# A hybrid decoder trunk: forget sums carried into the scores by the keys' zero rows, the mask inside the minimum, query blocks taken last to first

## The chip, the cores and the metric

One Trainium2 chip, one of its cores. A time is the device time of one execution in microseconds (us), as the core's own clock gives it. Three executions of the kernel before took 1271.95, 1272.39 and 1273.62 us; 1272.39 is their median. A separate, profiled execution gives the trace. TensorE is PE in the profile, its weight load PEld, VectorE DVE, ScalarE ACT, GpSimd POOL, and SyncE SP (here it only issues DMAs).

## What is computed

Two decoder layers over 16 meta tokens and 512 real ones (T = 528 columns, features on the partitions), width 1024. In each layer one input projection feeds eight heads of forgetting attention (64 features each) and four retention heads (128 features each); their outputs go through one output projection, then a gated feed-forward part follows. The change lies in the attention:

```python
c = jnp.cumsum(logf, axis=1).transpose(0, 2, 1)          # one running sum for each head
s = jnp.einsum('bhqd,bhkd->bhqk', q_blk, k_).astype(jnp.float32) * scale
s = s + c_q[..., :, None] - c_k[..., None, :]
s = jnp.where(k_pos[None, :] <= q_pos[:, None], s, -jnp.inf)
p = jax.nn.softmax(s, axis=-1)
return jnp.einsum('bhqk,bhkd->bhqd', p.astype(v_.dtype), v_)
```

A softmax over keys is not changed by a term that is the same for all keys of a query, so the kernel needs only the keys' sums `c_k`. The four real query blocks hold 128 queries each; block b (0 to 3) reads 16 + 128 (b + 1) keys: 144, 272, 400 or 528. The meta queries are block -1 (16 queries, 16 keys), present in layer 0 alone, since layer 1 drops the meta outputs.

## The kernel before

All products use fp32 split into a rounded high part and the remainder (`split`, L142: ACT rounds, DVE subtracts), so a dense product is three matmuls (L218), in layer 0 on two halves of 264 columns, in layer 1 on 512 columns where meta columns aren't needed. Weights come by SP's DMA queue into three buffers `raw`, are rounded by ACT (L192) and subtracted by POOL or DVE (L195) one or two jobs ahead.

The order of PE is written out by hand: `layer` (L1247) builds a list of steps, and `merge` (L247) puts placed steps between base steps, a place being the number of the base step that it stands behind. The order of DVE, ACT, POOL and SP follows from a scheduler at build time, and each of these engines works strictly in that order; PSUM tiles for the placed steps come from a pool of four (`psum_a`, L260).

The front of layer 0 (L1316): the first dense steps of q and k of head pair 0, interleaved (16 steps, `qk`), then `first_parts`, the gates' matmuls (L381), the sums of squares (L291) that give R, the row norm (L296 to L301), then the delayed ends of q and k (`q_done`, `k_done`) around `forget_sums`, then v. `forget_sums` (L391) makes the running sum by a scan (L401), writes it to DRAM (`cdr`, L403), and the first `scores` step of each head reads one row of it back to all 128 partitions (`bc`, L501). Both DMAs stand in SP's queue, between the loads of weights.

`fox_steps` (L474) are the placed steps of one head pair g: for each of its two heads s, and for block -1, 0, 1, 2, 3 in that order, `scores` then three steps later `turn`; `values` after the second score; `product(0)` and `product(1)`. In detail:

- `q_done` (L430): `qs` of head s holds the rounded queries in the head's 64 rows and their remainder in the other 64.
- `k_done` (L444): `kh` holds the rounded keys in both halves; `kl` the keys' remainder in the head's half, zero in the other half (zeroed once for each layer, L85). Two matmuls (L511) with `qs` then give all three terms.
- `scores` (L496): the two matmuls for each segment, the mask added to the diagonal 128 columns in PSUM by DVE (L517), one DVE instruction that takes `bc` minus score, writes it and its minimum (L518), and ACT's Exp (L531) with the row's sum. Block 3 has 528 keys and so two segments of 264, two PSUM tiles and two L518.
- `turn` (L550): PE transposes the block's weights (L420), ACT and DVE split them into `pth` and `ptl` (L143, L144).
- `product` (L569): the products with values (L584) over five groups of keys j = 0 to 4; group j = 0 spans all 512 query columns and stands first.

A group's placed steps stand between the dense steps of retention head g and of head pair g + 1; for g = 0 the scores begin behind base step 7 and end at 31 (L1329). The end of the program (L1178 to L1231) takes the final norm over the last 240 columns: squares on ACT, their sum on DVE, split, five matmuls with ones (L1159), a root, three DVE instructions, four output multiplies (L1137), with DMAs to the output.

Of the kernel before, what the change touches and what calls it, by code (L numbers as in the profile page):

```python
# [10 lines left out]
F32 = mybir.dt.float32  # L11
F32R = mybir.dt.float32r
# [27 lines left out]
def hybrid_kernel(ctx, tc, x_t, w_in, w_fl, w_out, w_gate, w_up, w_down, vecs, b_fg, rope, decay, mask, ident, out_t):  # L40
# [13 lines left out]
    msk = const.tile([128, 128], F32, name="msk")  # L54
# [12 lines left out]
    p_tiles, t_tiles, pm_tiles, v_tiles, end_tiles, low_keys = [], [], [], [], [], []  # L67
# [13 lines left out]
    def enter_att(l):  # L81
        enter("att")
        low_keys[:] = [phase["att"].tile([128, T], F32R, name=f"kl{s}") for s in range(2)]
        for s, t in enumerate(low_keys):
            (nc.gpsimd if l else nc.vector).memset(t[64 * (1 - s):64 * (2 - s)].bitcast(F32), 0.0)  # L85
# [283 lines left out]
    def forget_gates(l, st):  # L369
        if l:  # L370
            load_gates(l, st)
            gate_weights(l, st)
        else:
            for t, src in ((bfg, b_fg), (msk, mask), (idt, ident)):
                nc.sync.dma_start(t, src)
        wf = st["wf"]
# [14 lines left out]
    def forget_sums(l, st):  # L391
# [10 lines left out]
        st["cdr"] = tc.dram_tile([FH, T], F32, name=f"cdr{l}")  # L402
        nc.sync.dma_start(st["cdr"], z2)  # L403
# [20 lines left out]
    def fox_dense(l, g, ly, real, st):  # L424
# [5 lines left out]
        def q_done(ps):  # L430
# [4 lines left out]
            for s in range(2):  # L435
# [3 lines left out]
                nc.scalar.copy(sv(t, real, a0, a1), sv(tq, real, a0, a1))  # L439
                nc.vector.tensor_sub(sv(t, real, b0, b1), sv(tq, real, a0, a1), sv(t, real, a0, a1).bitcast(F32))  # L440
                st["q"].append(t)


        def k_done(ps):  # L444
# [3 lines left out]
            for s in range(2):  # L448
                kh = at(f"kh{s}")
                kl = low_keys[s]  # L450
                a0, a1 = ROWS[s]
                for b0, b1 in (ROWS[s], ROWS[1 - s]):
                    nc.scalar.copy(kh[b0:b1, :], tk[a0:a1, :])
                nc.vector.tensor_sub(kl[a0:a1, :], tk[a0:a1, :], kh[a0:a1, :].bitcast(F32))
                st["k"].append((kh, kl))
# [18 lines left out]
    def fox_steps(g, st, ly, real):  # L474

        blocks = list(range(0 if real else -1, NBLK))
# [19 lines left out]
        def scores(s, b):  # L496
            nq, nk, q0 = span(b)
            if b == blocks[0]:
                bc = at("bc", F32, bufs=2)
                hd = 2 * g + s  # L500
                nc.sync.dma_start(bc, ly["cdr"][hd:hd + 1, :].partition_broadcast(128))  # L501
                st["bc"] = bc
            bc = st["bc"]
# [4 lines left out]
            for c0, c1 in segs:  # L508
                sc = psum_a()
                for i, kk in enumerate(st["k"][s]):  # L510
                    nc.tensor.matmul(sc[0:nq, 0:c1 - c0], st["q"][s][:, q0:q0 + nq], kk[:, c0:c1],  # L511
# [913 lines left out]
```

## Time and profile before

| | us |
|---|---|
| median of three executions | 1272.39 |
| lowest, highest | 1271.95, 1273.62 |
| span of the profiled execution, first to last instruction | 1270.1 |
| what lies around the span (median less span) | 2.3 |
| PE busy in the span | 1252.6 (99%) |
| DVE, ACT, POOL busy | 1003.8, 694.5, 263.3 |
| granted TensorE clock, mean of the span | 0.996 |

The profiled execution is another than the three timed ones; its own time is known as its span, and the 2.3 us around it is taken from the median. A busy PE isn't a PE at its peak, as matmuls overlap: one that is issued every 0.12 us shows 0.28 us. So PE's waits are read from the list of who waited for whom, from the timeline, and from the granted clock in a stretch. The chain that ended last, the part 4 of the page, follows the work back from the last instruction.

### The profile page before, as it was taken

What the parts mean: (1) busy time and instruction counts of PE and PEld (TensorE: products, weight loads), DVE (VectorE), ACT (ScalarE), POOL (GpSimd) and SP (SyncE); (2) the same over time, 40 slices, a digit from 0 to 9 for tenths busy, and PEclk for the clock granted to TensorE, in tenths of its full rate; (3) what the DMA queues carried; (4) which work ended last, traced back from release to release, by engine and by line L of the source; (5) the groups of instructions that cost most, each with busy time, mean ns of one, the idle gap of its engine ahead of it and who ended that gap; (6) DMA issues with size and microseconds to landing.
All of it is one profiled execution on the core that took longest, in us unless ns stands there. A gap on an engine that the chain in (4) does not pass through costs nothing.

```text
span 1270.1 us, 23589 instructions
## 1 busy us (share of the span) xinstructions
PE 1252.6 (99%) x9225; PEld 1193.1 (94%) x9225; DVE 1003.8 (79%) x1866; ACT 694.5 (55%) x1284; POOL 263.3 (21%) x524
## 2 busy tenths in 40 slices
PE   9999999999999999999999999999999999999997
PEld 8899999999999999999998989998789999999996
DVE  7877856879988888887786877568899888888867
ACT  7666556676444444444465665457764444444445
POOL 3355546420000000000025546454100000000000
PEclk9999999999999999999999999999999999999999
DMA  6322222213323232322323122221223333333321
GB/s 218 93 68 84 83 94 75 68 68 116 106 96 100 100 100 100 100 100 84 101 76 114 63 101 84 77 91 67 100 91 126 101 100 101 100 100 100 100 84 67
DMA packets 45679, 120.56 MB, mean 95 GB/s; under 512 B 5360, under 2 KB 12272, under 8 KB 45568
## 3 DMA queue, kind: packets, MB, share of 16 engines
q1 hardware_dynamic: 45136, 118.77, 28.3%
q8 instruction: 72, 1.18, 0.4%
q14 instruction: 39, 0.32, 0.1%
q10 hardware_dynamic: 432, 0.29, 0.1%
HBM read 116.91 MB, written 2.13 MB: 94 GB/s over the span
## 4 chain that ended last, share of the span: by engine, by line
PE 89%; DVE 5%; ACT 4%; DMA 1%; issue 1%; ACTq 0%; DVEq 0%; SPq 0%
PE psd L218 27%; PE psa L902 18%; PE psd L1037 14%; PE psd L902 13%; PE psa L218 5%; PE psa L1037 4%; PE psa L420 2%; PE psa L511 1%; PE psa L584 1%; PE psa L717 1%; PE psa L751 1%; DMA bc<-cdr 1%; PE psa L381 1%; ACT whi L192 1%; DVE pr L518 0%
## 5 line engine op out<-in xcount | busy, mean ns | idle before, releaser
L195 POOL TENSOR_TENSOR wlo<-raw,whi 128x128 fp32r<-128x128 f32 x504 | 259.1, 550 | 288.8 <-ACT whi L192 287.3
L218 PE MATMUL psd<-xh,whi 128*128 128x264 f32 (+1 forms) x792 | 195.6, 314 | 0.4 <-ACT whi L192 0.4
L218 PE MATMUL psd<-xl,whi 128*128 128x264 f32 (+1 forms) x792 | 186.3, 302 | 0.6 <-DVE xl L321 0.6
L218 PE MATMUL psd<-xh,wlo 128*128 128x264 f32 (+1 forms) x792 | 186.7, 303 | 0.0
L218 PEld LDWEIGHTS psd<-xh,whi 128*128 128x128 f32 x792 | 128.2, 189 | 5.2 <-ACT whi L192 0.8
L218 PEld LDWEIGHTS psd<-xh,wlo 128*128 128x128 f32 x792 | 127.0, 188 | 6.3 <-DVE wlo L195 0.6
L218 PEld LDWEIGHTS psd<-xl,whi 128*128 128x128 f32 x792 | 127.6, 189 | 5.2 <-DVE xl L321 1.2
L192 ACT CAST whi<-raw 128x512 fp32r<-128x512 f32 (+1 forms) x168 | 98.2, 613 | 45.7 <-PE psd L218 31.5
L890 ACT CAST whi<-raw 128x1024 fp32r<-128x1024 f32 (+2 forms) x62 | 54.8, 884 | 50.3 <-PE psd L902 37.0
L890 ACT CAST fwhi<-raw 128x1024 fp32r<-128x1024 f32 (+2 forms) x62 | 55.6, 897 | 47.9 <-PE psd L902 40.1
L891 DVE TENSOR_TENSOR fwlo<-raw,fwhi 128x1024 fp32r<-128x1024 f32 (+2 forms) x62 | 64.0, 1032 | 11.7 <-ACT fwhi L890 11.6
L85 POOL MEMSET kl<- 64x528 f32 x2 | 1.1, 534 | 345.5 <-PE psa L902 345.5
L891 DVE TENSOR_TENSOR wlo<-raw,whi 128x1024 fp32r<-128x1024 f32 (+2 forms) x62 | 62.9, 1014 | 12.2 <-ACT whi L890 12.1
L902 PE MATMUL psa<-th,whi 128*128 128x264 f32 (+1 forms) x232 | 65.4, 282 | 0.0
L902 PE MATMUL psa<-th,wlo 128*128 128x264 f32 (+1 forms) x232 | 65.4, 282 | 0.0
L902 PE MATMUL psa<-tl,whi 128*128 128x264 f32 (+1 forms) x232 | 65.3, 282 | 0.0
L902 PE MATMUL psa<-th,fwhi 128*128 128x264 f32 (+1 forms) x224 | 63.4, 283 | 0.0
L902 PE MATMUL psa<-tl,fwhi 128*128 128x264 f32 (+1 forms) x224 | 63.3, 283 | 0.0
L902 PE MATMUL psa<-th,fwlo 128*128 128x264 f32 (+1 forms) x224 | 63.2, 282 | 0.0
L531 ACT ACTIVATE pr<-pr,nmax 128x144 f32<-128x144 f32 (+1 forms) x64 | 36.9, 576 | 43.2 <-DVE nmax L518 31.2
L890 ACT CAST fwhi<-S 128x1024 fp32r<-128x1024 f32 x20 | 21.0, 1049 | 68.6 <-PE psa L902 66.5
L968 ACT COPY e<-psa 128x264 f32<-128x264 f32 (+1 forms) x114 | 42.9, 376 | 27.7 <-PE psa L902 23.6
(356 smaller groups left out, 4036.6 us busy)
## 6 DMA issues: line engine op xcount, KB each, us to landing
raw<-w_in SPq DMA_DIRECT2D x54, 512.0 KB, 3.5
raw<-w_gate SPq DMA_DIRECT2D x44, 512.0 KB, 4.0
fraw<-w_up SPq DMA_DIRECT2D x38, 512.0 KB, 3.4
raw<-w_down SPq DMA_DIRECT2D x64, 256.0 KB, 2.7
raw<-w_out SPq DMA_DIRECT2D x16, 512.0 KB, 3.4
raw<-w_down SPq DMA_DIRECT2D x32, 192.0 KB, 2.5
bc<-cdr SPq DMA_DIRECT2D x16, 264.0 KB, 3.4
raw<-w_up SPq DMA_DIRECT2D x6, 512.0 KB, 3.5
```

The source lines that it names most:

```text
L192: pin(nc.scalar.copy(hi, job["raw"][:, c0:c1]), pinned)
L195: pin(sub(lo[:, c:c + step], job["raw"][:, c0 + c:c0 + c + step], hi[:, c:c + step].bitcast(F32)), pinned)
L218: nc.tensor.matmul(ps[1][b][:, 0:c1 - c0], w[:, wk, :], x[:, c0:c1], start=(k == 0 and i == 0), stop=(k == n - 1 and i == 2))
L381: nc.tensor.matmul(ps[:, 0:c1 - c0], wf[k // HB][:, k % HB, :], st["x"][k][part][:, c0:c1], start=(i == 0), stop=(i == 2 * NK - 1))
L420: nc.tensor.transpose(ps[:, 128 * j:128 * j + 128], src[:, o:o + 128], idt)
L511: nc.tensor.matmul(sc[0:nq, 0:c1 - c0], st["q"][s][:, q0:q0 + nq], kk[:, c0:c1], start=(i == 0), stop=(i == 1))
L531: nc.scalar.activation(pr, pr, AF.Exp, bias=nmax[0:nq], scale=-1.0, accum_out=rsum)
L890: nc.scalar.copy(hi, src)
L891: nc.vector.tensor_sub(lo, src, hi.bitcast(F32))
L902: nc.tensor.matmul(bank()[:, 0:b.shape[-1]], a[:, o + k, :], b, start=(fresh and k == 0 and i == 0), stop=(k == n - 1 and i == 2), skip_gr ...
L968: nc.scalar.copy(self.t["e"][:, i], self.t["x"][:, 0:w])
L1037: nc.tensor.matmul(v[:, 0:c1 - c0], a[:, s * n + k, :], b[:, c0:c1], start=(k == 0 and i == 0), stop=(k == n - 1 and i == 2))
```

## The change

It has four parts.

1. **The running sum as contraction rows.** The scan's result is rounded into rows 0 to 7 of a small tile `fs` (ACT), its remainder goes to rows 32 to 39 (DVE). For each head one instruction multiplies `fs` by a column of `pick` (ones at row hd and row 32 + hd) into 40 rows of the half of `kc` that holds no keys: on DVE for g = 0, on POOL for g > 0. `kc` (rounded keys and these rows) meets `qo` (rounded queries, and ones in the other half); `kx` (rounded keys in one half, remainder in the other) meets `qs`. Two matmuls for each segment, as before. `cdr`, `bc` and their 18 DMAs go. ACT rounds each head's queries twice (`qo` and `qs`).
2. **The mask in the minimum.** `msk` is now 528 wide, zero but for the last 128 columns, and takes the place of `bc` in the DVE instruction; the 72 separate adds go.
3. **Order.** Blocks run 3, 2, 1, 0 (and -1); the products with values run j = 4 to 0, the first with `start`, the narrow ones first. For layer 0, g = 0 the scores' places are 10.5 to 32.5. In layer 0's front the last two of the sixteen q and k steps stand behind the gates' matmuls.
4. **The end.** The sum of squares of the last columns goes unsplit into a fp32 matmul (no ACT rounding, no DVE subtraction); `out_a(2)` moves from behind step 4 to behind step 7.

```diff
-    msk = const.tile([128, 128], F32, name="msk")
+    msk = const.tile([128, T], F32, name="msk")
+    nc.vector.memset(msk[:, 0:T - 128], 0.0)
+    pick = const.tile([32 + FH, FH], F32, name="pick")
...
-        low_keys[:] = [phase["att"].tile([128, T], F32R, name=f"kl{s}") for s in range(2)]
-        for s, t in enumerate(low_keys):
-            (nc.gpsimd if l else nc.vector).memset(t[64 * (1 - s):64 * (2 - s)].bitcast(F32), 0.0)
+        for s in range(2):
+            rest = slice(64 * (1 - s), 64 * (2 - s))
+            zero(l, k_tiles[s][rest].bitcast(F32))
+            (nc.gpsimd if l else nc.vector).memset(q_tiles[s][rest].bitcast(F32), 1.0)
+        zero(l, f_tiles[0].bitcast(F32))
...
-        st["cdr"] = tc.dram_tile([FH, T], F32, name=f"cdr{l}")
-        nc.sync.dma_start(st["cdr"], z2)
+        with ExitStack() if l else tc.high_priority():
+            nc.scalar.copy(f_tiles[0][0:FH], z2)
+            nc.vector.tensor_sub(f_tiles[0][32:32 + FH], z2, f_tiles[0][0:FH].bitcast(F32))
...
-                nc.scalar.copy(sv(t, real, a0, a1), sv(tq, real, a0, a1))
-                nc.vector.tensor_sub(sv(t, real, b0, b1), sv(tq, real, a0, a1), sv(t, real, a0, a1).bitcast(F32))
+                for o in (q_tiles[s], t):
+                    nc.scalar.copy(sv(o, real, a0, a1), sv(tq, real, a0, a1))
+                nc.vector.tensor_sub(sv(t, real, b0, b1), sv(tq, real, a0, a1), sv(q_tiles[s], real, a0, a1).bitcast(F32))
...
-                for b0, b1 in (ROWS[s], ROWS[1 - s]):
-                    nc.scalar.copy(kh[b0:b1, :], tk[a0:a1, :])
-                nc.vector.tensor_sub(kl[a0:a1, :], tk[a0:a1, :], kh[a0:a1, :].bitcast(F32))
+                nc.scalar.copy(kc[a0:a1, :], tk[a0:a1, :])
+                nc.scalar.copy(kx[b0:b1, :], tk[a0:a1, :])
+                nc.vector.tensor_sub(kx[a0:a1, :], tk[a0:a1, :], kc[a0:a1, :].bitcast(F32))
+                hd = 2 * g + s
+                (nc.gpsimd if g else nc.vector).tensor_scalar(kc[b0:b0 + 32 + FH, :], f_tiles[0].bitcast(F32), pick[:, hd:hd + 1], 0.0, ALU.mult, ALU.add)
...
-        blocks = list(range(0 if real else -1, NBLK))
+        blocks = list(range(NBLK - 1, -1 if real else -2, -1))
...
-                nc.sync.dma_start(bc, ly["cdr"][hd:hd + 1, :].partition_broadcast(128))
...
-                    if c1 == nk:
-                        diag = sc[0:nq, c1 - c0 - nq:c1 - c0]
-                        nc.vector.tensor_add(diag, diag, msk[0:nq, 0:nq])
-                    nc.vector.tensor_tensor_reduce(pt[0:nq, c0:c1], sc[0:nq, 0:c1 - c0], bc[0:nq, c0:c1],
+                    nc.vector.tensor_tensor_reduce(pt[0:nq, c0:c1], sc[0:nq, 0:c1 - c0], msk[0:nq, m0 + c0:m0 + c1],
...
-            for j in range(5):
+            for j in range(4, -1, -1):
...
-                                     start=(j == 0 and i == 0), stop=(j == 4))
+                                     start=(j == 4), stop=(j == 0 and i == 1), skip_group_check=True)
...
-                out_a(2)
                 scale_b(1)
...
-                hi, lo = tt("sqh", F32R)[:, 0:nb], tt("sql", F32R)[:, 0:nb]
-                pin(nc.scalar.copy(hi, fin["acc"]))
...
-                sums(v, (fin["one"][0], hi, lo, fin["one"][1], fin["one"][2]))
+                sums(v, [fin["one"][0], fin["acc"]] + fin["one"][1:])
+                out_a(2)
                 out_a(4)
...
-            plan += [lambda: squares(ly, FULL, True, False)] + qk[:6] + qk[6:] + [first_parts] + gates + stats + [lambda: ly["wait"].pop(0)()] + sums + [lambda: ly["wait"].pop(0)()]
+            plan += [lambda: squares(ly, FULL, True, False)] + qk[:-2] + [first_parts] + gates + qk[-2:] + stats + [lambda: ly["wait"].pop(0)()] + sums + [lambda: ly["wait"].pop(0)()]
...
-            m0, r0, places = (((7, 31), (34, 40.5), (13, 33.5, 35.5, 37.5, 39, 40.5, 43, 44, 47.5, 48)),
+            m0, r0, places = (((7 if l else 10.5, 31 if l else 32.5), (34, 40.5), (13, 33.5, 35.5, 37.5, 39, 40.5, 43, 44, 47.5, 48)),
```

PE's count of matmuls stays but for the end (two rounded ones become one fp32 one). DVE loses 72 adds, ACT gains 16 roundings of queries and 2 of `fs`, POOL gains 12 instructions of 40x528, and SP loses 18 DMAs.

How the scheduler now lays out the other engines is shown at three places. First DVE in layer 0, from the gates' arithmetic to the first score (ISA is the minimum instruction, `pd` are value tiles, `z` the gates and their sum). Before:

```order
L400 TENSOR_TENSOR z<-z_424,z 8x528
L460 SCALAR_TENSOR_TENSOR pd_107<-psa,R 128x264
L401 SCALAR_TENSOR_TENSOR z_424<-z 8x528
L454 TENSOR_TENSOR kl_101<-tq,kh_438 64x528
L454 TENSOR_TENSOR kl_102<-tq,kh_442 64x528
L460 SCALAR_TENSOR_TENSOR pd_107<-psa,R 128x264
L1259 SCALAR_TENSOR_TENSOR sr<-sr,R 128x528
L517 TENSOR_TENSOR psa<-psa,msk 16x16
L639 SCALAR_TENSOR_TENSOR pd_108<-psd,R 128x528
L517 TENSOR_TENSOR psa<-psa,msk 128x128
L518 ISA pm_116,nmax<-psa,bc 16x16
```

Now, from the same arithmetic of the gates:

```order
L408 TENSOR_TENSOR z<-z_435,z 8x528
L465 TENSOR_TENSOR kx_447<-tq,kc_105 64x528
L409 SCALAR_TENSOR_TENSOR z_435<-z 8x528
L465 TENSOR_TENSOR kx_452<-tq,kc_106 64x528
L1258 SCALAR_TENSOR_TENSOR sr<-sr,R 128x528
L412 TENSOR_TENSOR fs<-z_435,fs 8x528
L644 SCALAR_TENSOR_TENSOR pd_116<-psd,R 128x528
L467 TENSOR_SCALAR kc_105<-fs,pick 40x528
L467 TENSOR_SCALAR kc_106<-fs,pick 40x528
L523 ISA pr,nmax<-psa,msk 128x264
```

The scan (L401, now L409) stands at the same point, but the remainder of `fs`, `sr`, the retention values and the two writes of `kc` now stand between it and the first score's minimum, and the first score's matmul needs `kc` as well.

Second ACT over the same stretch: the roundings of queries and keys, and the gates' three functions between them. Before:

```order
L439 CAST qs_418<-tq 64x528
L439 CAST qs_421<-tq 64x528
L396 ACTIVATE z_424<-z,bfg 8x528
L397 ACTIVATE z_424<-z_424 8x528
L398 ACTIVATE z_424<-z_424,onec 8x528
L453 CAST kh_438<-tq 64x528 x2
L453 CAST kh_442<-tq 64x528 x2
```

Now (the first row in front of these is the rounding into `qo_103`):

```order
L449 CAST qs_427<-tq 64x528
L404 ACTIVATE z_435<-z,bfg 8x528
L449 CAST qo_104<-tq 64x528
L405 ACTIVATE z_435<-z_435 8x528
L449 CAST qs_431<-tq 64x528
L406 ACTIVATE z_435<-z_435,onec 8x528
L463 CAST kc_105<-tq 64x528
L464 CAST kx_447<-tq 64x528
L463 CAST kc_106<-tq 64x528
L464 CAST kx_452<-tq 64x528
```

Two more roundings stand ahead of the gates' last function, and the rounding into `fs` stands behind all of these and one small copy.

Third DVE around `product(0)` of layer 0, g = 0 (`xsw`, `rkl` and the `tq` belong to the retention keys' rotation; `mixt` is the product's output). Before:

```order
L627 TENSOR_TENSOR xsw<-xsw,sr 128x528
L517 TENSOR_TENSOR psa<-psa,msk 128x128
L629 TENSOR_TENSOR tq<-psd,cr 128x528
L518 ISA pr,nmax<-psa,bc 128x400
L518 ISA nmax 128x1
L630 TENSOR_TENSOR tq<-tq,xsw 128x528
L144 TENSOR_TENSOR ptl<-psa,pth 128x4x128
L579 TENSOR_TENSOR mixt<-psa,ol 64x16
```

Now, from the last `ptl` of the head to the product's output:

```order
L632 TENSOR_TENSOR xsw<-xsw,sr 128x528
L634 TENSOR_TENSOR tq<-psd,cr 128x528
L151 TENSOR_TENSOR ptl<-psa,pth 128x128
L635 TENSOR_TENSOR tq<-tq,xsw 128x528
L523 ISA pr,nmax<-psa,msk 128x144
L523 ISA nmax 128x1
L564 TENSOR_TENSOR pth<-pm,pth 16x16
L151 TENSOR_TENSOR rkl<-tq,rkh 128x528
L540 STREAM_TRANSPOSE pe<-pr 32x128
L544 RECIPROCAL sums<-sums 128x8
L584 TENSOR_TENSOR mixt<-psa,ol 64x16
```

The last `ptl` ahead of the product was the widest (512 columns) and stood directly in front of it; it is now the narrowest (128) and several instructions stand between.

More of the change, by code (lines that the diff above doesn't have):

```diff
@@ L373, in forget_gates @@
         else:
-            for t, src in ((bfg, b_fg), (msk, mask), (idt, ident)):
+            for t, src in ((bfg, b_fg), (idt, ident), (msk[:, T - 128:T], mask)):
                 nc.sync.dma_start(t, src)
+            nc.vector.tensor_add(pick, idt[0:32 + FH, 0:FH], idt[0:32 + FH, 32:32 + FH])
         wf = st["wf"]
@@ L509, in scores @@
                 sc = psum_a()
-                for i, kk in enumerate(st["k"][s]):
-                    nc.tensor.matmul(sc[0:nq, 0:c1 - c0], st["q"][s][:, q0:q0 + nq], kk[:, c0:c1],
+                for i, (qq, kk) in enumerate(zip(st["q"][s], st["k"][s])):
+                    nc.tensor.matmul(sc[0:nq, 0:c1 - c0], qq[:, q0:q0 + nq], kk[:, c0:c1],
                                      start=(i == 0), stop=(i == 1))
@@ L532, in scores @@
             info[s, b] = pt
-            if b == blocks[-1]:
+            if b == 0:
                 st["ends"] = at("pe", F32, (32, NBLK, 32), 2)
@@ L562, in turn @@
                 split(pth[:, j0:j0 + n, q0:q0 + nq], ptl[:, j0:j0 + n, q0:q0 + nq], p3[:, :, 0:nq])
-            if b == blocks[-1]:
+            if b == 1:
                 e = st["ends"][0:META, :, 32 - META:32]
```

32 lines of the change are left out of this document (14 added, 18 removed).

## The prediction

> **What bounds the kernel now.** I read the page first: the busy times, and the chain that ended last by engine.
>
> ```profile
> PE 1252.6 (99%) x9225; PEld 1193.1 (94%) x9225; DVE 1003.8 (79%) x1866; ACT 694.5 (55%) x1284; POOL 263.3 (21%) x524
> ...
> PE 89%; DVE 5%; ACT 4%; DMA 1%; issue 1%; ACTq 0%; DVEq 0%; SPq 0%
> ```
>
> PE sets the end, and the change leaves PE's list of matmuls as long as it was. So it can gain only what PE now waits for, and lose only by new waits of PE. What DVE loses (72 adds) or ACT gains (18 roundings) counts only where PE stands waiting. The list of PE's waits gives the whole stock (total us, times, longest):
>
> ```profile
> PE psa L584 <- DVE ptl L144: 1.7, 1, 1.7
> ...
> PE psa L420 <- DVE vv L488: 1.6, 1, 1.6
> PE psa L1159 <- ACT S L1130: 0.7, 1, 0.7
> PE psa L511 <- DVE mixt L588: 0.7, 1, 0.7
> PE psa L511 <- DVE kl L454: 0.6, 1, 0.6
> PE psa L751 <- DVE rsl L144: 0.6, 2, 0.4
> PE psa L511 <- DVE nmax L518: 0.6, 1, 0.6
> ```
>
> All of it is a few us of 1270. From start to start each wait costs about 0.2 us more than is listed, because a matmul lasts 0.28 us in the profile and is issued every 0.12 us. So the gains in reach are near 1.9, 1.8 and 0.8 us, and 0.2% (2.5 us, about what a measurement of this kernel can tell from no change) is not reached by one of them. The table by stretches adds one thing (span, PE busy, granted clock, DMA share, GB/s):
>
> ```profile
> 56.00:59.00 3.00, 1.31 (x10) 1.00 0.00 0
> 59.30:62.72 3.41, 3.41 (x16) 0.50 0.46 154
> ...
> 677.00:681.00 4.00, 2.43 (x15) 1.00 0.37 122
> ```
>
> After the 1.7 us wait at `product(0)` the clock stood at half for 3.41 us, which costs another 1.7 us. After the 1.6 us wait at 678 us it did not fall. A wait of this length can cost twice what it shows, and whether it does is not settled by its length alone.
>
> [...]
>
> **Terms that leave.** *The wait at the first product.* The third place shown by the order: in front of `product(0)` stood the widest `ptl`, behind the rotation's three instructions. Now the narrowest stands there, with other work between, and the product takes its narrow groups first. I take the wait (1.9) and the half clock behind it (1.7) as gone: 3.6 us. If the rotation still holds up the last `ptl`, nothing of it is gained.
>
> *The wait at the values in layer 1.* The chain of waits shows where it comes from:
>
> ```profile
> 669.27 0.33 SPq L159
> 669.60 0.05 issue
> 669.65 2.94 DMA cdr<-z
> 672.59 0.02 issue
> 672.60 3.22 DMA bc<-cdr
> ```
>
> SP works in order, and `cdr` was issued only behind a load of weights that waited for its buffer; with 2.94 and 3.22 us the row sums reached DVE at 676, after the first score. Without these DMAs the sums come by ACT and DVE, before layer 1's first score. I take 1.8 us; at least 1.0, because the scores of 528 keys now come first and hold two PSUM tiles.
>
> *The wait for `kl`* in layer 0 (0.8 from start to start) goes too, replaced by what follows. *The wait behind the gates*: moving the last two q and k steps behind the gates' matmuls gives ACT and DVE 1.5 us of PE work (12 matmuls of 0.12) to empty the gates' PSUM tiles. It was
>
> ```profile
> 22.99 0.19 PEld L218 LDWEIGHTS psa<-xh,mxh 128*128 128x128 f32 x1 [0.60 <-DVE z L388]
> ```
>
> 0.6 us at the weight load, 0.8 from start to start; I take all of it.
>
> *The end* (DVE):
>
> ```profile
> 1258.76 0.72 DVE L1137 TENSOR_TENSOR th<-th,e 128x544 f32<-128x544 f32 x1
> ...
> 1260.56 0.41 DVE L1215 TENSOR_TENSOR sql<-S,sqh 128x240 fp32r<-128x240 f32 x1
> 1260.89 0.40 DVE L1095 TENSOR_TENSOR h<-psa,h 128x240 f32<-128x240 f32 x1
> 1261.21 1.35 DVE L1137 TENSOR_TENSOR th<-th,e 128x544 f32<-128x544 f32 x2
> 1262.98 0.41 DVE L1151 TENSOR_TENSOR S<-S 128x240 f32<-128x240 f32 x1 [0.43 <-ACT S L1147]
> ```
>
> The last add into h (1260.89) stands behind one output multiply and the subtraction; without both it starts about 1.1 us sooner, and the root with it. But the multiply now stands behind it, so that three of 0.65 to 0.7 follow it before the three final instructions, which DVE reaches at about 1262.1 instead of 1262.98. I take 0.9 us (0.3 if ACT's squares become the later ones, 1.3 if DVE catches up).
>
> **Terms that come.** *The start.* DVE zeroes two half tiles first; it now fills four, the 40 rows of `fs` and the wide mask:
>
> ```profile
> 1.72 1.14 DVE L85 MEMSET kl<- 64x528 f32 x2 [0.16 <-issue]
> ...
> 5.72 0.42 DVE L195 TENSOR_TENSOR wlo<-raw,whi 128x256 fp32r<-128x256 f32 x1 [0.47 <-ACT whi L192]
> 6.51 0.43 DVE L195 TENSOR_TENSOR wlo<-raw,whi 128x256 fp32r<-128x256 f32 x1 [0.37 <-ACT whi L192]
> 7.16 0.77 DVE L321 SCALAR_TENSOR_TENSOR xl<-h,vec,xh 128x528 fp32r<-128x528 f32 x1 [0.21 <-ACT xh L320]
> ```
>
> Four more at about 0.5 is 2.0 us, of which an idle time for a DMA there hides 0.5 or more. Of the 1.5 left the gaps of 0.47, 0.37 and 0.21 take up 1.05. I take 0.45 us (0 to 1.5).
>
> *The first score of layer 0.* It needs `kc` with the sums in it, where before only DVE needed `bc`. ACT and DVE work as the first two places show. ACT before:
>
> ```profile
> 28.11 1.29 ACT L439 CAST qs<-tq 64x528 fp32r<-64x528 f32 x2 [2.91 <-DVE tq L433]
> 29.42 0.74 ACT L396 ACTIVATE z<-z,bfg 8x528 f32<-8x528 f32 x1
> ...
> 32.32 2.60 ACT L453 CAST kh<-tq 64x528 fp32r<-64x528 f32 x4 [0.72 <-DVE tq L446]
> ```
>
> and DVE, with the end of R and the prices of a TENSOR_SCALAR on few rows and of a plain instruction over 528 columns:
>
> ```profile
> 26.45 0.89 DVE L301 SCALAR_TENSOR_TENSOR R<-nwt,R 128x528 f32<-128x528 f32 x1
> ...
> 31.10 0.58 DVE L399 TENSOR_SCALAR z<-z,bfg 8x528 f32<-8x528 f32 x1
> 31.60 0.69 DVE L446 SCALAR_TENSOR_TENSOR tq<-psd,R 128x528 f32<-128x528 f32 x1
> ```
>
> R ends at 27.34 and ACT starts 0.77 later. From there it has four roundings of queries (0.645 each, 2.6), three functions (0.74 at most, 2.2), four of keys (2.6), a small copy (0.2) and the rounding into `fs` (0.65, by the row of the keys): R + 9.0. DVE then has the remainder of `fs`, the retention values and the first TENSOR_SCALAR (about 0.65, 0.65, 0.6), and `sr` ends 0.4 after ACT: R + 11.2. R itself comes later: ACT's list now has three roundings of weights ahead of the norm's first function, where one stood among its functions. With 0.5 us for one more, R ends near 27.9 and the score may start at 39.1 (38.5 with no shift, 39.7 with two). PE arrives as follows:
>
> ```profile
> 29.20 0.40 PE L218 MATMUL psd<-xh,whi 128*128 128x264 f32 x2
> ...
> 34.27 0.17 PE L511 MATMUL psa<-kh,qs 128*16 128x16 f32 x1
> ```
>
> Seven base steps took 5.07 us, so eleven take 8.0: 37.2, less the 0.8 behind the gates, with the start's 0.45: 36.9. PE waits 2.2 us (1.6 to 2.8). Behind that matmul PE's whole list is queued, so all of it counts; on DVE the first minimum and the values are behind it. A wait of 2.2 us is longer than the 1.7 us that halved the clock: 1.7 us more, taken as likely.
>
> **Edits at no cost.** The wider mask in the minimum: same instruction, same columns, another operand. The 72 adds were
>
> ```profile
> L517 DVE TENSOR_TENSOR psa<-psa,msk 128x128 f32<-128x128 f32 (+1 forms) x72 | 19.9, 277 | 10.8 <-PE psa L511 10.6
> ```
>
> 19.9 us of DVE beside PE's work; what they cost PE is in the waits. The queries' second rounding is 1.3 us of ACT for each group, eight dense steps (5.8 us) before the keys' end; if ACT is behind there, the next group's first score waits up to 1.3 us. POOL's 12 instructions on 40x528 aren't in the trace. The nearest rows are
>
> ```profile
> L195 POOL TENSOR_TENSOR wlo<-raw,whi 128x128 fp32r<-128x128 f32 x504 | 259.1, 550 | 288.8 <-ACT whi L192 287.3
> ...
> L85 POOL MEMSET kl<- 64x528 f32 x2 | 1.1, 534 | 345.5 <-PE psa L902 345.5
> ```
>
> so 0.5 us by the fill and 2.3 by columns (528 / 128 x 0.55); I take 1.0, nearer the fill. They stand between pieces of weights made several dense steps ahead, on an engine that idles 288.8 us before such pieces; without that cover each would hold PE up by its own length. The order of the blocks adds no work.
>
> **The sum**, against the span of 1270.1 us and 2.3 around it: - 3.6 (product) - 1.8 (values) - 0.8 (`kl`) - 0.8 (gates) - 0.9 (end) + 0.45 (start) + 2.2 + 1.7 (first score) = - 3.55. From the median, 1272.39, that is 1268.8 us.
>
> **Rivals.** *The first score costs less*: the clock stays up, as after 678 us, or the chain to `kc` is shorter. Then 1.7 to 3.9 us of the new term go: 1264.9 to 1267.1. For it: half of the two waits near 1.7 us left the clock alone. Against: 2.2 is longer than both. *The waits only move*: PE's order is fixed, DVE works in order, and what waited at the product waits at the next PSUM tile instead. Then the product's 3.6 us aren't gained: 1272.4. For it: the listed waits for `mixt` and `nmax` are waits for a tile. *Slower*: at each head of a group the 528-key block now comes first, with two tiles of the pool of four, two minimum instructions and the longest Exp, just before the transposes of the values, which want two more. From the point where DVE is 2.5 us late there (`values` follows the first score by that in the later groups), PE waits for a tile. The nearest price is the wait for `nmax` at such a head, 0.8 from start to start; at the seven other heads 5.6 us, and one more half clock 1.7: 1276.1. Against it: DVE has 2.5 us less work in each group.
>
> **Chances.** Forecast 0.48 (its own range 1267.2 to 1270.8), first score cheaper 0.24, waits that move 0.10, slower at the heads 0.18. Faster by over 0.2% is below 1269.85: 0.34 of the forecast and the 0.24, together 0.58. Slower than 1274.93: most of the last, and 0.03 of the third: 0.20. Within: 0.22. The range that leaves out about 0.2 reaches from 1264.5 (cheapest first score, with the best end) to 1273.0, which takes in the waits that move.
>
> **What would show it.** A PE wait of 1.6 to 2.8 us for `kc` near 37 us and a half clock behind it; no PE wait for `ptl` at the first `product(0)`, none for `vv` in layer 1; DVE's final three instructions 0.9 us sooner, counted from PE's last dense matmul. The forecast is wrong if PE waits at the later groups' first scores or values, or if the sum of its waits isn't smaller.

## The result and the profile after

The changed kernel took 1276.77 us (median of five, 1276.43 to 1277.68), the kernel before, on the same chip, 1272.16 (1270.85 to 1273.62). The ratio is 1.0038, with a 95% interval from 1.0026 to 1.0049: **slower by 0.38%, 4.6 us**. The forecast was 1268.8 and its range ended at 1273.0; it was wrong. The profiled execution is the slowest of the five (1277.68 us). Its span is 1275.9 us where the one of before had 1270.1, so in the traces 5.8 us are to be found.

The page of the changed kernel: the busy times, and the chain that ended last by engine.

```profile
PE 1254.7 (98%) x9225; PEld 1195.6 (94%) x9225; DVE 995.6 (78%) x1804; ACT 705.2 (55%) x1301; POOL 274.8 (22%) x539
...
PE 87%; DVE 6%; ACT 5%; issue 1%; DMA 1%; DVEq 0%; SPq 0%; ACTq 0%
```

DVE lost 8 us of work, ACT and POOL gained 11 each, and none of that set the end. What did is in the list of PE's waits (total us, times, longest):

```profile
PE psa L519 <- DVE kc L467: 3.1, 1, 3.1
PE psa L429 <- DVE mixt L584: 3.0, 1, 3.0
PE psa L1277 <- DVE wide L63: 2.0, 1, 2.0
PE psa L756 <- DVE rsl L151: 1.3, 3, 0.7
PE psa L519 <- DVE ptl L151: 0.8, 1, 0.8
PE psa L722 <- DVE ptl L151: 0.7, 1, 0.7
PE psa L581 <- DVE pth L564: 0.5, 1, 0.5
PE psd L225 <- DVE tq L442: 0.5, 1, 0.5
```

The 1.7 us for `ptl` at the first product and the 1.6 for `vv` in layer 1 are gone. In their place stand two waits of 3 us, for `kc` at the first score (forecast) and for `mixt` at 242 us (not forecast). Behind the start PE's waits add up to 11.1 us where they were 7.5, which the forecast had named as a sign of being wrong. The stretches around both (length, busy times, granted clock, DMA share, GB/s):

```profile
38.26:41.68 3.42, 0.35 (x4) 0.37 (x4) 3.29 (x5) 1.19 (x4) 3.01 (x6) 1.00 0.01 2
41.68:45.09 3.41, 3.41 (x17) 3.40 (x16) 1.76 (x8) 1.00 (x3) 1.28 (x3) 0.50 0.30 74
243.06:246.48 3.42, 0.80 (x7) 0.83 (x8) 3.38 (x8) 1.97 (x6) 1.83 (x4) 1.00 0.17 20
246.48:249.89 3.41, 3.41 (x18) 3.34 (x17) 2.17 (x4) 0.46 (x1) 0.00 (x0) 0.50 0.35 138
```

Behind each wait PE ran 3.41 us at half clock (0.50 in the rows), half of which, 1.7 us, was lost each time. Before, there was one such stretch.

Both traces hold 3408 dense matmuls (L218, now L225) in almost the same order. So the start of the n-th in one trace less its start in the other says where the time went:

| at (us, before) | after less before | what lies in front of it |
|---|---|---|
| 9.3 | +0.5 | the start |
| 29.2 | +0.9 | R later, PE waits for `tq` |
| 50.4 | +5.1 | first score with its half clock |
| 62.9 | +1.8 | the first product no longer waits, no half clock there |
| 104.8 | +5.8 | small waits from 62 us on; some steps moved ahead of this point |
| 230.7 | +5.0 | |
| 248.4 | +9.0 | the wait for `mixt` and its half clock |
| 676.9 | +8.9 | |
| 682.8 | +7.2 | values of layer 1 |
| 945.9 | +6.4 | |
| end | +5.8 | the end |

The wait at 242 us in PE's timeline (start, duration, instruction, and in brackets the idle time and what ended it):

```profile
239.71 0.41 PE L298 MATMUL psa<-sqh,ones 128*128 128x264 f32 x2
...
240.94 0.17 PE L581 MATMUL psa<-pth,vv 128*128 128x16 f32 x1
240.97 0.42 PE L589 MATMUL psa<-pth,vv 128*128 128x16 f32 x2
...
242.24 0.40 PE L589 MATMUL psa<-ptl,vv 128*128 128x512 f32 x1
245.68 0.63 PE L429 MATMUL psa<-idt,pr 128*128 128x128 f32 x4 [3.05 <-DVE mixt L584]
```

and what DVE does there:

```profile
244.53 0.92 DVE L305 TENSOR_TENSOR nwt<-r 128x528 f32<-128x528 f32 x1
245.38 0.16 DVE L584 TENSOR_TENSOR mixt<-psa,ol 64x16 f32<-64x16 f32 x1
245.46 0.67 DVE L593 TENSOR_TENSOR mixt<-psa,ol 64x512 f32<-64x512 f32 x1
246.06 0.75 DVE L307 SCALAR_TENSOR_TENSOR nwt<-psa,nwt 128x264 f32<-128x264 f32 x2
```

Layer 0's retention head 2 sends its sums of squares into two PSUM tiles (L298). DVE empties them only at 246.06 (L307). The product takes the other two tiles (L581 and L589). With blocks going down, the next step is the transposes of block 3 (L429), directly behind the product, and they want a fifth tile. With blocks going up, that step was block -1, whose `turn` gives PE nothing, and eighteen dense matmuls (three base steps, 2.3 us) stood there before PE wanted two more tiles. The kernel before, at the same place:

```profile
237.43 0.22 PE L584 MATMUL psa<-pth,vv 128*128 128x16 f32 x1
...
239.53 0.41 PE L218 MATMUL psd<-xh,wlo 128*128 128x264 f32 x2
239.78 0.28 PE L511 MATMUL psa<-kh,qs 128*128 128x264 f32 x1
...
240.87 0.39 PE L511 MATMUL psa<-kh,qs 128*128 128x264 f32 x1 [0.69 <-DVE mixt L588]
```

### The profile page after: what moved, and what is told of

It is laid out like the page before. It is cut to its first block, busy times and chain, and to the rows that moved or that the text cites. A ratio compares the mean times of both kernels' runs of the same rounds, so it can differ in the third digit from the quotient of the medians.

```text
span 1275.9 us, 23525 instructions
## 1 busy us (share of the span) xinstructions
PE 1254.7 (98%) x9225; PEld 1195.6 (94%) x9225; DVE 995.6 (78%) x1804; ACT 705.2 (55%) x1301; POOL 274.8 (22%) x539
## 3 DMA queue, kind: packets, MB, share of 16 engines
q1 hardware_dynamic: 42800, 114.41, 27.9%
## 4 chain that ended last, share of the span: by engine, by line
PE 87%; DVE 6%; ACT 5%; issue 1%; DMA 1%; DVEq 0%; SPq 0%; ACTq 0%
PE psd L225 26%; PE psa L907 18%; PE psd L1042 14%; PE psd L907 13%; PE psa L225 5%; PE psa L1042 4%; PE psa L429 2%; PE psa L589 1%; PE psa L519 1%; PE psa L722 1%; PE psa L756 1%; DMA h<-x_t 1%; ACT whi L199 1%; PE psa L298 0%; DVE ptl L151 0%
## 5 line engine op out<-in xcount | busy, mean ns | idle before, releaser
L225 PE MATMUL psd<-xh,whi 128*128 128x264 f32 (+1 forms) x792 | 195.8, 315 | 0.5 <-DVE tq L442 0.5
L225 PE MATMUL psd<-xl,whi 128*128 128x264 f32 (+1 forms) x792 | 187.5, 304 | 0.4 <-DVE xl L328 0.4
L225 PE MATMUL psd<-xh,wlo 128*128 128x264 f32 (+1 forms) x792 | 187.8, 305 | 0.0
L225 PEld LDWEIGHTS psd<-xh,whi 128*128 128x128 f32 x792 | 129.7, 191 | 5.8 <-issue 0.8
L225 PEld LDWEIGHTS psd<-xh,wlo 128*128 128x128 f32 x792 | 128.2, 190 | 6.2 <-DVE wlo L202 0.4
L225 PEld LDWEIGHTS psd<-xl,whi 128*128 128x128 f32 x792 | 128.6, 190 | 5.0 <-DVE xl L328 1.0
L896 DVE TENSOR_TENSOR wlo<-raw,whi 128x1024 fp32r<-128x1024 f32 (+2 forms) x62 | 62.9, 1014 | 12.3 <-ACT whi L895 12.1
L536 ACT ACTIVATE pr<-pr,nmax 128x528 f32<-128x528 f32 (+1 forms) x64 | 36.8, 575 | 38.0 <-DVE nmax L523 20.0
```

The costliest lines, as they stand in the source:

```text
L225: nc.tensor.matmul(ps[1][b][:, 0:c1 - c0], w[:, wk, :], x[:, c0:c1], start=(k == 0 and i == 0), stop=(k == n - 1 and i == 2))
L536: nc.scalar.activation(pr, pr, AF.Exp, bias=nmax[0:nq], scale=-1.0, accum_out=rsum)
L896: nc.vector.tensor_sub(lo, src, hi.bitcast(F32))
```

## The experiments

Ratios are to the kernel before, run beside it on the same chip. The changed kernel also sets `dynamic_dma_scratch_size=1024` where the program is built, a line that the description of the change doesn't list. No run has it alone; e1_up keeps it and e4_down_alone lacks it, so it isn't what the order costs. Theory A: the new order of the blocks costs, through PSUM tiles at 242 us and small waits before 110. Its rival B: the row sums cost. C and its variants ask what makes `kc` late, D and F what the half clock and DVE's list are worth.

**e1_up: blocks up again.**

```diff
-        blocks = list(range(NBLK - 1, -1 if real else -2, -1))
+        blocks = list(range(0 if real else -1, NBLK))
...
-            for j in range(4, -1, -1):
+            for j in range(5):
```

> The changed kernel with its third part partly undone: blocks go up again (-1, 0 to 3) and the products with values take j from 0 to 4, in every group; the row sums, the mask, the places of the first group, the front and the end stay as changed. Theory A (the order of the blocks is what costs: the 3.2 us wait at 242 us of layer 0 with the half clock behind it, and the small waits between 47 and 110 us): the 4.1 us at 242 go, 2.9 us of small waits go, and the wait at the first product comes back with 1.3 us more and perhaps a half clock of 1.7; the wait for kc at 38 us stays. 1276.8 - 4.1 - 2.9 + 1.3 = 1271.1, or 1272.8 with the half clock. Theory B (the costs come from the row sums: more for ACT and DVE in each group, so the waits stay wherever the blocks stand): within 1 us of 1276.8.

Measured: 1269.8 us, ratio 0.9985 [0.9976, 0.9995]. The waits left in its trace:

```profile
PE psa L519 <- DVE kc L467: 3.1, 1, 3.1
...
PE psa L519 <- DVE mixt L593: 0.7, 1, 0.7
```

Theory A holds: by the ratios the order costs 0.53%, some 6.7 us. (The two profiled executions differ by 7.0 us, of which 0.8 stands at 30 us already, in a front that both kernels have alike.) The wait at 242 is back to the 0.7 of before. Two things the expectation had wrong: the first product doesn't wait either, and of the small waits from 47 to 110 us most stay (2.3 us from start to start, 3.2 in the changed kernel). Without the order the change is a little faster than before, in spite of the wait for `kc`.

**e2_norm_later: one place moved in the changed kernel.**

```diff
-                      ret_places(2, 26, 23.5, 24.5, 32, 28, 33.5, 36, 56.5, 40.5, 57.5),
+                      ret_places(2, 26, 23.5, 24.5, 32, 28, 33.5, 36, 56.5, 40.5 if l else 44, 57.5),
```

> The changed kernel with one place moved: in layer 0 the head norm of retention head 2, whose sums of squares hold two of the four PSUM tiles from 239.7 to 246.7 us, goes from place 40.5 to place 44, behind product(0) and the first turn of the second head. Theory A1 (the transposes at 242 us wait because four tiles are taken, two by these sums and two by the product that now stands directly ahead): the wait of 3.2 us and the half clock of 1.7 us go, at most 0.8 comes back elsewhere: 1271.9 to 1272.7. Theory A2 (DVE itself is late there, by the new order, and any next tile would be waited for): the wait moves and less than 1.5 us is gained: 1275.3 to 1276.8.

Measured: 1272.46 us, ratio 1.0009 [0.9999, 1.0019], 4.3 us less than the changed kernel (3.7 by the ratios). PE's timeline there, with no idle time in front of the transposes:

```profile
241.21 0.39 PE L589 MATMUL psa<-ptl,vv 128*128 128x512 f32 x1
241.44 0.60 PE L429 MATMUL psa<-idt,pr 128*128 128x128 f32 x4
241.80 0.49 PE L225 MATMUL psd<-xh,whi 128*128 128x264 f32 x2
```

A1 holds: with two tiles free nobody waits there, though DVE has as much to do. The length of the wait has a second cause: in the changed kernel the norm's functions on ACT and one of its DVE instructions (L305) stand ahead of the add that frees a tile (L584, at 245.38), and in e2 that add comes at 242.39. With all tiles taken, but this work out of the way, the wait would have been about 1 us by these rows, an estimate.

**e4_down_alone: the order alone, on the kernel before.** The diff is that of e1_up the other way round.

> The kernel before with the order alone: blocks 3, 2, 1, 0 (and -1), products with values j = 4 to 0; sums by way of DRAM, the separate mask, front, places and end as before. Theory A (the order costs): 4.1 us at the last group of layer 0 and about 2.9 of small waits come, the first product's 1.3 us and its half clock of 1.7 go: 1272.2 + 4.1 + 2.9 - 3.0 = 1276.2, from 1274.5 to 1277.9. Theory B (the row sums cost, the order does not): the product's wait and half clock go and nothing comes: 1269.2.

Measured: 1278.75 us, ratio 1.0054 [1.0036, 1.0072], above the range of A: the profiled execution ran at half clock for three times 3.41 us, twice behind the wait at 240 us (239.59 to 246.41) and once behind that at 687 us (686.73 to 690.15), where A counted one. Its waits:

```profile
PE psa L420 <- DVE mixt L579: 3.2, 1, 3.2
PE psa L420 <- DVE nmax L518: 2.3, 3, 1.2
PE psa L420 <- DVE vv L488: 1.9, 1, 1.9
```

The order brings the 3.2 us by itself. It also brings waits of the values' transposes for tiles held by the two segments of block 3 (`nmax`, at 38 and 681 us), the mechanism of the prediction's slower rival. In the changed kernel, where no sums come by way of DRAM, they don't occur.

**e3_pool_round: ACT spared of two roundings.**

```diff
-                    nc.scalar.copy(sv(o, real, a0, a1), sv(tq, real, a0, a1))
+                    (nc.gpsimd.tensor_copy if (l, g) == (0, 0) and o is t else nc.scalar.copy)(sv(o, real, a0, a1), sv(tq, real, a0, a1))
```

> The changed kernel with the second rounding of the queries (qs) of the first group of layer 0 made by POOL as a copy of qo, where ACT made it; nothing else. DVE's row up to the first score then has the retention values and half of the values behind the two writes of kc. Theory C1 (kc is late because ACT and DVE have more to do between R and kc than PE): kc comes 1.3 to 1.8 us sooner, so PE waits 1.4 to 1.9 us in place of 3.2, and the half clock behind it may stay or go: 1273.3 to 1275.5. Theory C2 (DVE is busy without a gap from R to kc, so what ACT is spared counts for nothing and only the 0.7 us of one moved DVE instruction is gained): 1276.1, with a wait of 2.5 us and the half clock.

Measured: 1275.63 us, ratio 1.0032 [1.0019, 1.0045]; PE still waits 2.6 us for `kc`, with the half clock. The time lies between the two theories (C1 ended at 1275.5, C2 said 1276.1); the wait is C2's number: ACT's list isn't what sets `kc`. POOL's copies didn't hide a gain, since beside them DVE's instructions took 0.4 us more at most. The changed kernel's DVE shows why; behind its row at 26.35 us no row up to 42 us has an idle time in brackets:

```profile
28.23 0.89 DVE L308 SCALAR_TENSOR_TENSOR R<-nwt,R 128x528 f32<-128x528 f32 x1
...
30.75 0.69 DVE L1258 SCALAR_TENSOR_TENSOR cr<-cr,R 128x528 f32<-128x528 f32 x1
...
36.17 1.24 DVE L409 TENSOR_TENSOR_SCAN z<-z 8x528 f32<-8x528 f32 x1
37.44 0.71 DVE L465 TENSOR_TENSOR kx<-tq,kc 64x528 fp32r<-64x528 f32 x1
38.18 0.71 DVE L1258 SCALAR_TENSOR_TENSOR sr<-sr,R 128x528 f32<-128x528 f32 x1
38.92 0.85 DVE L412 TENSOR_TENSOR fs<-z,fs 8x528 fp32r<-8x528 f32 x1
39.80 0.71 DVE L644 SCALAR_TENSOR_TENSOR pd<-psd,R 128x528 f32<-128x528 f32 x1
40.54 1.26 DVE L467 TENSOR_SCALAR kc<-fs,pick 40x528 fp32r<-40x528 f32 x2
```

**e10_rope_pool and e12_no_rope: DVE spared of `cr` and `sr`.** e10 gives the two products to POOL, e12 leaves them out in layer 0.

```diff
-                nc.vector.scalar_tensor_tensor(t, t, RSC, ly["R"], ALU.mult, ALU.mult)
+                if l == 0:
+                    nc.gpsimd.tensor_scalar_mul(t, t, RSC)
+                    nc.gpsimd.tensor_mul(t, t, ly["R"])
+                else:
+                    nc.vector.scalar_tensor_tensor(t, t, RSC, ly["R"], ALU.mult, ALU.mult)
```

> The changed kernel, with layer 0's two products of the rotation tables with R (cr and sr, 0.69 and 0.71 us of DVE between R and kc) made by POOL, and their constant factor by POOL ahead of R; nothing else. Theory C2 (DVE, busy without a gap from R to kc, sets the time of kc): kc comes 1.4 us sooner, PE waits 1.8 us in place of 3.2: 1275.4; if the half clock goes with it, 1273.7. Theory C1 (ACT's list sets it): less than 0.5 us, 1276.3 or more.

> The changed kernel without layer 0's two products of the rotation tables with R: the tables are used as they come from memory, so this part of the computation is left out, and no engine makes it. DVE's row up to the first score is that of e10_rope_pool. There POOL made the two products in 2.8 us, and two DVE instructions beside it (L407, L450) took 1.25 and 1.40 us where they take 0.48 and 0.70. Theory F (DVE's list without a gap sets the time of kc, and in e10_rope_pool POOL's work slowed DVE by the 1.4 us that it was spared): now kc comes 1.4 us sooner, the wait is 1.8 us: 1275.4, and 1273.7 if the half clock goes with it. Theory G (DVE's list does not set it): 1276.5 or more, wait 3.0 as in e10_rope_pool.

Measured: e10 1276.8 us, ratio 1.0043 [1.0028, 1.0058], with a wait of 3.0 for `kc`, which taken alone is C1's number; e12 1274.27 us beside 1270.38 of before, ratio 1.0033 [1.0021, 1.0046], with a wait of 1.8. The time of e12 doesn't separate F from G, since 1.4 us is within its interval. The wait does: 1.8 is F's number. The n-th dense matmul at 50 us starts 2.3 us sooner than in the changed kernel; 0.8 of that stands at 36 us already, ahead of the wait, so 1.4 us remain. The rows of e10 where DVE's gain went, POOL's work and the two DVE instructions beside it:

```profile
32.08 1.32 POOL L1260 TENSOR_TENSOR cr<-cr,R 128x528 f32<-128x528 f32 x1
33.37 1.52 POOL L1260 TENSOR_TENSOR sr<-sr,R 128x528 f32<-128x528 f32 x1
```

```profile
32.44 1.25 DVE L407 TENSOR_SCALAR z<-z,bfg 8x528 f32<-8x528 f32 x1
33.62 0.41 DVE L473 SCALAR_TENSOR_TENSOR pd<-psa,R 128x264 f32<-128x264 f32 x1
34.06 1.40 DVE L450 TENSOR_TENSOR qs<-tq,qo 64x528 fp32r<-64x528 f32 x1
```

In e12, in the same order on DVE and with POOL idle there, they are short again:

```profile
31.54 0.47 DVE L407 TENSOR_SCALAR z<-z,bfg 8x528 f32<-8x528 f32 x1
...
32.39 0.70 DVE L450 TENSOR_TENSOR qs<-tq,qo 64x528 fp32r<-64x528 f32 x1
```

So `kc` comes when DVE has worked off its list: beside POOL's two products L407 and L450 took 0.78 and 0.70 us longer than in e12, as much as the 1.4 us that DVE was spared.

**e6_warm: PE kept busy while it waits for `kc`.**

```diff
+        def warm():
+            idle = psum_a()
+            for _ in range(11):
+                nc.tensor.matmul(idle, ones, ly["x"][0][0][:, 0:512], start=True, stop=True)
...
+                          [] if l or g else [(10.4, warm)],
```

> [...] Theory D1 (the half clock from 41.7 to 45.1 us comes because PE stood idle ahead of it): the clock stays at 1, the score starts when it did, 1.7 us are gained: 1275.1. Theory D2 (the half clock has another cause, such as PE's load before it): half clock as before, 1276.8.

Measured: 1275.78 us, ratio 1.0037 [1.0023, 1.005]. The eleven matmuls on 512 columns, whose results nothing reads, took 2.73 us in the trace. The times alone don't tell 1.0 us from none. The trace does: the wait is 0.5 us, and the clock is 1 where it was at half:

```profile
39.00:42.00 3.00, 2.50 (x16) 1.95 (x16) 2.82 (x8) 0.22 (x1) 3.00 (x7) 1.00 0.00 0
42.00:46.00 4.00, 3.75 (x32) 3.54 (x30) 2.70 (x8) 2.28 (x7) 0.28 (x1) 1.00 0.42 131
```

At 50 us its dense matmuls are 2.1 us ahead of the changed kernel's, and 0.7 us at 36 us, ahead of the wait; so 1.4 of the 1.7 us show there (D1).

**e5_up_later, e7_place_alone, e8_down_fixed: places.** e5 is e1_up, and e8 the changed kernel with e2's edit, each with the first group's scores later:

```diff
-            m0, r0, places = (((7 if l else 10.5, 31 if l else 32.5),
+            m0, r0, places = (((7 if l else 15, 31 if l else 33.5),
```

e7 is the kernel before with the changed kernel's places for that group (10.5 to 32.5).

> e1_up (blocks going up again) with the scores of the first group of layer 0 placed from 15 to 33.5 in place of 10.5 to 32.5, so that PE has 3.3 us more of dense work ahead of the first score. Theory C (PE's wait of 3.2 us for kc and the half clock of 1.7 us behind it are a pure loss of place): both go, 1269.8 - 4.9 = 1264.9, up to 1266.5 if the steps, now 1.0 base steps apart in place of 1.2, make PE wait for DVE at the retention head's steps around 46 to 72 us. Theory C2 (DVE has been the bound since R, and a later score only moves the wait): 1269 to 1270, with the same total of PE's waits before 75 us.

> The changed kernel, blocks going down, with both places moved: the head norm of e2_norm_later at 44 and the first group's scores from 15 to 33.5. If the two losses are independent: 1276.8 - 4.3 (measured for the head norm) - 4.9 (kc and the half clock) = 1267.6. If the order costs beyond the one place, it stays 2.7 us above e5_up_later, as e2_norm_later stood 2.7 above e1_up. If the descending order makes PE wait for tiles at the later place: 1270 or more.

> The kernel before with one number pair changed: the scores of the first group of layer 0 from 10.5 to 32.5 in place of 7 to 31, as in the changed kernel; order, sums, mask, front and end as before. Theory P1 (the waits of the kernel before at the first product, 1.9 with 1.7 of half clock, and at the first scores, 0.8 and 0.8, came from the place): 1272.2 - 5.2 = 1267.0, at least 1268.6. Theory P2 (they came from the order or from the sums by way of DRAM): 1272.2, with a wait for ptl at the first product.

Measured: e5 1266.63 us, ratio 0.9963 [0.995, 0.9976]; e8 1267.29, ratio 0.9968 [0.9957, 0.998]; e7 1271.34, ratio 1.0 [0.999, 1.0009]. In e5 and e8 nobody waits for `kc` and the clock stays up to the last matmuls. e5 lies just above C's range: PE waits 0.8 to 1.0 us at 40, 50 and 65 us instead. e8 met the number for independent losses. Two things follow. With the places moved the descending order loses nearly all that it cost: e8 is 0.7 us above e5, with intervals that overlap. And the place alone does nothing for the kernel before, whose first product still waits 1.3 us for `ptl` (P2).

**e9_up_norm and e11_all: the best of it.** e9 is e5 with e2's edit. e11 adds e10's edit and the start's fills on POOL:

```diff
-    nc.vector.memset(msk[:, 0:T - 128], 0.0)
+    nc.gpsimd.memset(msk[:, 0:T - 128], 0.0)
...
-            (nc.gpsimd if l else nc.vector).memset(q_tiles[s][rest].bitcast(F32), 1.0)
+            nc.gpsimd.memset(q_tiles[s][rest].bitcast(F32), 1.0)
...
-        zero(l, f_tiles[0].bitcast(F32))
+        nc.gpsimd.memset(f_tiles[0].bitcast(F32), 0.0)
```

> e5_up_later with the head norm of layer 0's retention head 2 at place 44 in place of 40.5, as in e2_norm_later. Tile theory: its 0.87 us of wait for mixt at 238 us, which the kernel before has too, goes, with no half clock to gain: 1266.6 - 0.9 = 1265.7. Rival (with rising blocks the later norm takes its tiles from the scores behind it): 1266.6 or up to 1 us more.

> e9_up_norm with e10_rope_pool's edit and, at the start, the fills of msk, qo and fs on POOL in place of DVE. Start: 0.5 us back (the trace has the changed kernel's dense matmuls 0.46 us later by the 24th). Front: the waits for tq, pd and the like at 29 and 39 us, 1.3 in e5_up_later, lose up to 1.0. 1265.7 - 0.5 - 0.7 = 1264.5 (1264.0 to 1265.2). Rival: POOL's fills delay its parts of the first weights, then the start gains nothing: 1265.

Measured: e9 1265.62 us, ratio 0.9954 [0.9938, 0.9971]; e11 1265.38, ratio 0.9952 [0.9937, 0.9966]. e9 beats both kernels, by 0.5% and 0.8%, and met its number. It is the like of e8, both places moved and blocks going up, and stands 1.7 us below it; the intervals overlap, so whether the descending order still costs that much isn't settled. e11 adds nothing that can be measured: it missed its 1264.5 and stands nearer its rival's 1265.

## Why the prediction was wrong

By its own steps, with sizes from the two traces (start to start):

| step | forecast | measured |
|---|---|---|
| wait at the first product | -1.9 | -1.3 (1.94 before; 0.67 left) |
| half clock behind it | -1.7 | -1.7 |
| values of layer 1 | -1.8 | -1.8 |
| `kl` | -0.8 | -0.8 |
| wait behind the gates, with the wait for `tq` that follows | -0.8 | +0.4 |
| end | -0.9 | -0.8 |
| start | +0.45 | +0.5 |
| first score waits for `kc` | +2.2 | +3.2 |
| half clock behind it | +1.7 | +1.7 |
| order of the blocks, at 242 us | 0 | +4.1 (3.2 less 0.85, and 1.7 of half clock) |
| order of the blocks, second head's block of 528 keys at 108 us | 0 | +0.9 |
| other small waits from 47 to 110 us, in e1_up too | 0 | +2.0 |
| others (`nmax` at 38.8 us gone, `rsl` later) | 0 | -0.5 |
| sum | -3.55 | +5.9 (the spans differ by 5.8) |

These are two single executions. The row of the gates is the one that moves most: in the eight other traces with the same front (e1, e2, e3, e5, e6, e8, e9 and e12) it is between -0.6 and +0.3.

The step that failed is the sentence "The order of the blocks adds no work", under the edits at no cost. It is true, and beside the point: the order took away dense matmuls that stood between two steps which share four PSUM tiles. e1_up and e2_norm_later show it, the first for the order as a whole, the second for the tiles at 242 us. e1_up's 1269.8 us lies in the forecast's own range, so most of the miss is this one term. Of the small waits, those for `pth` at the first product and for `ptl` at 108 us are in the traces of the changed kernel and of e2, e3, e6, e10 and e12, where blocks go down, and not in e1_up's. The other 2.0 us stand at the retention head's steps (46 to 72 us), beside the first group's new places; e7_place_alone has such a wait for `sq` too (1.2 us). They weren't taken apart further.

It could have been read from the program. The last group of layer 0 has 19 placed steps from 2 to 46.5, 2.47 apart. `product(0)`, the 16th, is put 0.8 of a step late, at 41.06; the next step stands at 41.56. No base step lies between. Going up, that next step was `turn` of block -1, empty on PE; going down it is `turn` of block 3, four transposes. The prediction looked at the first group's product only, and at DVE's row, where PE's row was the one that changed.

The slower rival had the right mechanism, a wait for a tile, and the wrong place. It priced the heads of the groups; in the changed kernel PE waited at none of the seven others, and for 0.8 us at one second head's block (108 us), while in e4_down_alone, where `bc` comes by DMA, it waited at such places for up to 1.2 us.

The 3.0 us gained at the first product (3.6 forecast) came for more than the reason given. The forecast put them down to the order; e4_down_alone, with the order alone, loses that wait, but so does e1_up, where blocks go up. So the order is enough and isn't needed, and here a number came out nearly right without its reason being shown.

The first score was right in kind and half clock, and 1.0 us too small. R ended at 29.12 and not at 27.9: ACT's three roundings of weights stood ahead of the norm's function, as foreseen, but took 1.66 us where 0.5 was allowed; in the eight other traces R ends between 28.24 and 28.65, so 0.5 to 0.9 us of the lateness is this execution's. It cost little by itself, since PE's dense work ahead of the score ended 1.2 us late too. What was too small is the way from R to the first score: 12.1 us (in e1_up and e2_norm_later too) where 11.2 had been worked out along ACT's list. ACT's rounding into `fs` ended at R + 8.95, as worked out; behind it DVE took 3.1 us to `kc` where 2.2 had been counted, because DVE worked without a gap from 26.35 us on, with `cr`, `sr` and the retention values between (e3_pool_round, e12_no_rope). The late R also took back the gates' gain in this trace: PE waits for `tq`, since the queries' PSUM tile can't be emptied without R.

Not settled: what the row sums, the mask and the end bring apart from one another. Together, with places that fit (e5_up_later), they bring 0.4%; no kernel here has only one of them.

## What to carry to other kernels

A reordering that adds no work still changes which steps are neighbours: for each pair of new neighbours on the bounding engine, count the buffers that both hold and the work that stood between them, in every group and not only in the first. Where a result must arrive early, find the engine whose list has no gap up to it, and price the chain by that list. Here two roundings taken from ACT left 2.6 of the 3.1 us of waiting (e3_pool_round), and two products given to POOL left 3.0, with two DVE instructions beside them 1.5 us longer (e10_rope_pool against e12_no_rope). When a step is moved, move its place with it: two places here were worth 9 us (e8_down_fixed).

## What the runs showed of the hardware

**Half clock came behind stretches with little matmul work.** In the changed kernel's trace the two half-clock stretches behind PE's waits lasted 3.413 us each; their front edges stand at 41.677 and 246.477 us, 60 such lengths apart. With steps of this length counted from such edges, and from 8 us on, the traces that have them show the following: a step at full clock in which PE was busy 1.76 us or less (1.76 in e10_rope_pool, in the step before 244 us) was followed by half clock, and one in which it was busy 1.84 us or more was not. No step lay between the two values. First the kernel before, at its two waits of 1.7 and 1.6 us:

```profile
55.89:59.30 3.41, 1.72 (x12) 1.35 (x11) 3.19 (x9) 2.34 (x7) 2.19 (x4) 1.00 0.00 0
677.11:680.52 3.41, 1.84 (x12) 1.45 (x11) 1.97 (x8) 1.92 (x8) 1.70 (x4) 1.00 0.30 96
```

then e12_no_rope, at its wait of 1.8 us (behind it the clock was at half from 40.51 to 43.92) and at the one of 3.0 us:

```profile
37.09:40.51 3.42, 1.63 (x14) 1.45 (x13) 3.26 (x8) 1.17 (x5) 3.04 (x6) 1.00 0.01 2
...
238.48:241.89 3.41, 1.88 (x13) 1.43 (x11) 2.46 (x5) 3.31 (x9) 3.41 (x7) 1.00 0.00 0
241.89:245.30 3.41, 1.92 (x16) 1.95 (x17) 3.38 (x8) 1.37 (x3) 0.70 (x2) 1.00 0.38 145
```

The 3.0 us wait fell across an edge, left 1.88 and 1.92 us of PE work in the two steps, and cost no half clock; in the changed kernel the same wait left 0.80 us of work in one step, and half clock followed. So the waits of 1.6 to 3.2 us in these traces cost a half clock in some places and none in others. e12's six times run from 1272.82 us (mean clock 0.999) to 1276.77 (0.994). That such waits fall differently in each execution would explain it, but only one execution of a kernel was traced, so this wasn't shown; and e1_up's ten times don't follow the clock (1269.24 us at 0.999, 1268.44 at 0.996).

Twice the half clock lasted two steps, in e4_down_alone (239.59 to 246.41) and in e10_rope_pool, where the 3.0 us wait lay across an edge and left 1.76 and 2.06 us of PE work on its two sides:

```profile
240.79:244.21 3.42, 1.76 (x12) 1.31 (x11) 2.61 (x5) 3.32 (x9) 3.42 (x7) 1.00 0.00 0
244.21:247.62 3.41, 2.06 (x10) 2.10 (x11) 3.38 (x8) 1.22 (x3) 0.55 (x2) 0.50 0.43 145
```

In both the first step at half clock had PE busy for part of the time, 2.06 us here and 2.56 in e4. Where the clock came back in the traces, PE had been busy for 3.13 us of the half-clock step (e6_warm, 243 to 247 us) or more.

**Two DVE instructions took longer beside POOL's products.** In e10_rope_pool, DVE's L407 and L450 took 1.25 and 1.40 us beside two POOL products of 1.32 and 1.52 us, and in e12_no_rope, without them, 0.47 and 0.70. L407 and L450 end 0.3 and 0.6 us after the POOL product during which they began. Not every instruction took longer: L473, which reads a PSUM tile, took 0.41 us during POOL's second product, as it does in e12. What held the two up wasn't shown.
